# Two hybrid blocks on one core: neighbourhood attention by heads instead of by column tiles, and two projections interleaved

## The chip, the cores and the metric

One core of a Trainium2 chip runs the whole program. The metric is the device time of one execution in microseconds. Of the kernel before there are three timed executions and one profiled one.

## The reference

A sequence of 512 rows of 1024 goes through two blocks. The first block is a gated linear recurrence and a sliding-window attention with 16 heads. The second block runs two attentions side by side, mixes them with gates, and ends in an MLP. In float32, shortened:

```python
z = rms_norm(x, norm_mix) @ w_in          # q_a k_a v_a q_b k_b v_b g_a g_b
y_a = windowed_gqa(q_a, k_a, v_a, sink)   # 8 heads of 64, 2 kv heads, |distance| <= 128, blocks of 128
y_b = neighborhood_attn(q_b, k_b, v_b, rpb)  # 8 heads of 64 over a grid of 8 x 64; 8 x 16 neighbours
gates = sigmoid(concat([g_a, g_b]) + b_gate)
merged = gates[:, :1024] * (y_a @ w_proj_a) + gates[:, 1024:] * (y_b @ w_proj_b)
x = x + merged @ w_out
x = x + square(relu(rms_norm(x, norm_mlp) @ w_up)) @ w_down
```

The grid of the neighbourhood attention has 8 rows, so every row sees all 8 rows, and only the 16 columns around its own.

## The kernel before

**Number form.** Each float32 operand of a product is split into a high part (`rb`, float32r) and the rest, a low part. A product is three matmuls (`mm3`: high x high, high x low, low x high) into one PSUM bank. `split` makes the two parts: the high one mostly on ACT, the low one on DVE.

**Order of the work.** The program is written as many small generators that yield operations. `Sched.run` (a list scheduler) picks among them by its own costs and priorities while the program is built and fixes the order of each engine. One generator, `main`, goes through the list of matrix products (`jobs`) strictly in order, for example `block2` for the second block. Attention units, evacuations and weight loads are generators of their own, whose operations fall between. `Slots` hands out the buffers: 62 slots of 128 x 512 in `rb`, 38 in `fb`, 8 PSUM banks. A generator that finds no free slots waits. Weights come by DMA into `fb`, become high (`hi_task`, POOL or ACT) and low (`lo_task`, DVE) in `rb`, in the order of the products.

**Attention.** `attn_unit` handles four score tiles of 128 queries at a time: Q·K on PE, mask and maximum on DVE, exp on ACT, 1/sum on POOL, transposes of the probabilities on PE, their split (ACT, DVE), then the products P·V (`pv`) and `evac`. At most `MAXU = 4` units are under way. For the sliding-window heads (`swa_unit`) and the windowed heads (`a_unit`) a unit is a group of four heads and one block of 128 queries. V lies there in two arrangements (`v_heads`, `dup`) so that heads of either half of the partitions come out in place, and P·V is done in two column halves of 256 (`pv_groups`).

The neighbourhood heads come in four pairs (`pr`). The 512 positions are sorted into four column tiles (`ct`) of 16 grid columns. The outer tiles 0 and 3 see two key tiles, the inner ones 1 and 2 see three. A unit (`b_unit`) is a pair of heads with either the two outer or the two inner tiles; each P·V there is three matmuls of 256 columns (high and low part of V by high and low part of P, without low x low).

**End of block 2.** `block2` runs the projections `w_pa` (of the windowed heads) and `w_pb` (of the neighbourhood heads), eight outputs of 128 rows each with four k-steps. `pa_evac` multiplies with the gate, `pb_evac` multiplies, adds both, and splits the merged row (STT line L360, TT line L346) for `w_out_2`. `gemm_open` opens several outputs with the first k-steps and finishes them later, so that the last pair of heads may come late.

Lines that the text speaks of: L396 matmuls, L420 transposes, L322 ACT, L331 POOL copy of weights, L346 DVE tensor_tensor, L360 DVE scalar_tensor_tensor, L374 POOL multiplication, L389 reciprocal, L980 mask and maximum, L426 DMA.

Of the kernel before, what the change touches and what calls it, by code (L numbers as in the profile page):

```python
# [247 lines left out]
def kernel(ctx: ExitStack, tc: tile.TileContext, io: dict, out: bass.AP):  # L248
# [704 lines left out]
    def attn_unit(cfg):  # L953

        inflight[0] += 1
        nk = cfg["nk"]
        nkb = nk // P
        np_ = 2 if nk <= 256 else 3
        pair = nk <= 256
# [51 lines left out]
        for h in range(4):  # L1011
            yield A(pt[:, h, 0:nk], pt[:, h, 0:nk], AF.Exp, bias=nm[:, h:h + 1], accum=dn[:, h:h + 1])
# [4 lines left out]
        for h in range(4):  # L1017
            yield PMUL(pt[:, h, 0:nk], pt[:, h, 0:nk], rc[:, h:h + 1])
# [847 lines left out]
```

## Time and profile before

| | us |
|---|---|
| timed executions | 1155.03, 1154.68, 1152.27 |
| median | 1154.68 |
| profiled execution, its own time | 1149.55 |
| span of the profiled execution | 1147.7 |
| PE busy | 1126.9 (98%) |
| PE weight loads busy | 942.2 (82%) |
| DVE busy | 758.6 (66%) |
| ACT busy | 385.9 (34%) |
| POOL busy | 296.1 (26%) |
| mean granted clock of TensorE | 0.995 |

How to read it: the engines work at the same time and each in its own fixed order. An engine that isn't the bound may wait at no cost. Matmuls are pipelined, so the busy time of a single one is longer than the distance between two. Rough places in the span: the recurrence to about 240, the sliding-window attention to about 405, its output projection and the start of block 2 to about 460, the attentions of block 2 to about 720, the end of block 2 to about 790, then the MLP.

### The profile page before, as it was taken

The numbers are of one execution on the slowest core, as the hardware profiler recorded it, in microseconds if no ns is written. First come the engines' busy times: TensorE is split into PE (matmuls) and PEld (weight loads), VectorE is DVE, ScalarE is ACT, GpSimd is POOL, SyncE is SP. The second block draws the span as 40 slices with busy tenths as digits, with TensorE's granted clock in tenths as the row PEclk, the third lists the DMA queues.
The fourth block names the chain that finished last, engine by engine and source line by source line (L and its number), as shares of the span: only waits on it lengthen the run. The fifth ranks groups of instructions, "written<-read, shape, count | busy, mean of one in ns | idle before, by whom it ended". The sixth has DMA issues, their size and how long they took to land.

```text
span 1147.7 us, 14995 instructions
## 1 busy us (share of the span) xinstructions
PE 1126.9 (98%) x5468; PEld 942.2 (82%) x5468; DVE 758.6 (66%) x1335; ACT 385.9 (34%) x782; POOL 296.1 (26%) x392
## 2 busy tenths in 40 slices
PE   9999999999999999999999999899999999999997
PEld 6788888888888778888888788688888888888887
DVE  7999999675787896657765554876654324555332
ACT  5456761234665621166352233211111111111101
POOL 1222332125577422034132222312110002112110
PEclk9999999999999999999999999999999999999999
DMA  7243445208222512811553452622333222233001
GB/s 287 87 127 107 130 137 193 74 1 239 53 91 88 167 63 56 239 56 56 170 162 86 147 150 88 198 82 94 92 110 128 93 76 91 85 97 110 1 1 74
DMA packets 46794, 125.86 MB, mean 110 GB/s; under 512 B 6272, under 2 KB 7936, under 8 KB 46720
## 3 DMA queue, kind: packets, MB, share of 16 engines
q1 hardware_dynamic: 46720, 124.90, 34.7%
q8 instruction: 43, 0.70, 0.3%
q14 instruction: 31, 0.25, 0.1%
HBM read 104.95 MB, written 2.10 MB: 93 GB/s over the span
## 4 chain that ended last, share of the span: by engine, by line
PE 87%; DVE 5%; DMA 2%; issue 2%; POOL 1%; ACT 1%; SPq 0%; POOLq 0%; DVEq 0%; ACTq 0%
PE ps L396 85%; PE ps L420 3%; DVE fb L360 2%; DVE rb L346 2%; DVE fb L346 1%; POOL fb L374 1%; DMA fb<-in_mk 1%; DMA rb<-rb 1%; DVE fb L980 0%; DMA fb<-in_w_out 0%; DVE rb L360 0%; ACT rb L322 0%; DMA fb<-in_x 0%; ACT fb L322 0%; SPq L426 0%
## 5 line engine op out<-in xcount | busy, mean ns | idle before, releaser
L396 PE MATMUL ps<-rb 128*128 128x512 f32 (+1 forms) x5008 | 1093.1, 377 | 11.8 <-DVE rb L360 3.7
L396 PEld LDWEIGHTS ps<-rb 128*128 128x128 f32 x5008 | 890.5, 189 | 186.0 <-DVE rb L360 5.8
L331 POOL TENSOR_SCALAR rb<-fb 128x1024 fp32r<-128x1024 f32 (+4 forms) x159 | 169.3, 1076 | 605.7 <-PE ps L396 465.5
L346 DVE TENSOR_TENSOR rb<-fb,rb 128x512 fp32r<-128x512 f32 (+5 forms) x301 | 285.9, 974 | 47.7 <-ACT rb L322 39.7
L322 ACT ACTIVATE rb<-fb 128x512 fp32r<-128x512 f32 (+4 forms) x134 | 99.0, 747 | 305.0 <-DVE fb L360 155.6
L346 DVE TENSOR_TENSOR fb<-ps,fb 128x512 f32<-128x512 f32 (+2 forms) x134 | 78.1, 584 | 155.4 <-PE ps L396 143.7
L346 DVE TENSOR_TENSOR fb<-fb 128x512 f32<-128x512 f32 (+1 forms) x120 | 89.7, 754 | 22.9 <-ACT rb L322 20.8
L374 POOL TENSOR_SCALAR fb<-fb,sm 128x256 f32<-128x256 f32 (+2 forms) x128 | 69.1, 561 | 116.3 <-DVE sm L389 97.1
L346 DVE TENSOR_TENSOR rb<-ps,rb 128x512 fp32r<-128x512 f32 (+1 forms) x92 | 58.6, 641 | 44.0 <-ACT rb L322 39.6
L322 ACT ACTIVATE rb<-ps 128x512 fp32r<-128x512 f32 (+1 forms) x92 | 50.9, 558 | 81.1 <-PE ps L420 63.3
L360 DVE SCALAR_TENSOR_TENSOR fb<-ps,fb 128x512 f32<-128x512 f32 x56 | 38.5, 687 | 59.2 <-PE ps L396 59.1
L322 ACT ACTIVATE fb<-fb,sm 128x256 f32<-128x256 f32 (+2 forms) x128 | 65.3, 512 | 28.0 <-DVE sm L368 23.5
L322 ACT ACTIVATE fb<-fb 128x512 f32<-128x512 f32 (+1 forms) x66 | 39.5, 612 | 92.4 <-DVE fb L346 73.2
L322 ACT ACTIVATE rb<-fb,vec 128x512 fp32r<-128x512 f32 x41 | 28.4, 719 | 103.1 <-DVE fb L346 101.1
L322 ACT ACTIVATE fb<-ps 64x256 f32<-64x256 f32 (+1 forms) x60 | 25.2, 423 | 79.7 <-PE ps L396 67.8
L420 PE MATMUL ps<-ident,fb 128*128 128x128 f32 x328 | 48.4, 272 | 1.3 <-DVE fb L1582 0.9
L420 PEld LDWEIGHTS ps<-ident,fb 128*128 128x128 f32 x328 | 39.4, 140 | 8.4 <-DVE fb L1582 1.1
L980 DVE CUSTOM_DVE_ANT_0 fb<-ps,fb 128x256 f32<-128x256 f32 (+1 forms) x64 | 28.6, 486 | 14.2 <-DMA fb<-in_mbe 7.3
L374 POOL TENSOR_SCALAR fb<-fb,sm_qt 128x256 f32<-128x256 f32 (+1 forms) x64 | 33.3, 546 | 2.2 <-DMA fb<-in_mk 2.1
L360 DVE SCALAR_TENSOR_TENSOR rb<-fb,vec,rb 128x512 fp32r<-128x512 f32 x41 | 30.5, 761 | 0.6 <-ACT rb L322 0.3
L360 DVE SCALAR_TENSOR_TENSOR fb<-fb,vec 128x512 f32<-128x512 f32 x36 | 30.8, 872 | 0.0
L980 DVE CUSTOM_DVE_ANT_0 fb<-ps,fb,sm_qs 128x256 f32<-128x256 f32 (+1 forms) x64 | 26.7, 444 | 5.7 <-PE ps L396 3.3
(83 smaller groups left out, 323.3 us busy)
## 6 DMA issues: line engine op xcount, KB each, us to landing
rb<-rb SPq DMA_DIRECT2D x128, 128.0 KB, 2.3
fb<-in_w_down SPq DMA_DIRECT2D x32, 512.0 KB, 3.7
fb<-in_w_in SPq DMA_DIRECT2D x31, 512.0 KB, 3.7
fb<-in_w_up SPq DMA_DIRECT2D x29, 512.0 KB, 3.5
fb<-in_a_w_in SPq DMA_DIRECT2D x22, 512.0 KB, 3.9
fb<-in_b_w_in SPq DMA_DIRECT2D x16, 512.0 KB, 4.6
fb<-in_a_w_out SPq DMA_DIRECT2D x8, 512.0 KB, 3.5
fb<-in_wg SPq DMA_DIRECT2D x8, 384.0 KB, 3.8
```

The costliest lines, as they stand in the source:

```text
L322: opts = [("ACT", dur, lambda: nc.scalar.activation(out=o, in_=i, func=fn, **kw), TABLES.get(fn))]
L331: lambda: nc.gpsimd.tensor_scalar(out=o, in0=i, scalar1=1.0, scalar2=1.0, op0=ALU.mult, op1=ALU.mult), None,
L346: lambda: nc.vector.tensor_tensor(out=o, in0=a, in1=b, op=op), None,
L360: lambda: nc.vector.scalar_tensor_tensor(out=o, in0=a, scalar=s, in1=b, op0=op0, op1=op1), None,
L374: lambda: nc.gpsimd.tensor_scalar(out=o, in0=a, scalar1=s, scalar2=1.0, op0=ALU.mult, op1=ALU.mult), None,
L396: nc.tensor.matmul(out=o, lhsT=l, rhs=r, start=st, stop=sp)
L420: nc.tensor.transpose(o, i, ident)
L980: nc.vector.tensor_tensor_reduce(out=pt[:, h, 0:nk], in0=PS[:, b, o0:o0 + nk], in1=m, scale=sc, scalar=-3.0e38, op0=ALU.add, op1=ALU.max, ...
```

## The change

1. **V in one arrangement.** `v_heads` makes the high parts of V and the low parts side by side (64 columns high, 64 low) and no second arrangement. So one P·V matmul yields high x P in one half of the partitions and low x P in the other, and `evac` adds the halves. `pv_all` does all 512 columns at once; `pv_groups` goes.
2. **Neighbourhood units by head.** `b_unit(pr, e)` is one head and all four column tiles. Its scores have 256, 384, 384 and 256 columns. Its transposes go by key tile (2, 3, 3 and 2 blocks). P·V takes V in the same one arrangement, key tile by key tile over the column tiles that see it; the first is widened to 512 columns, over zeros that POOL writes (`pad`). The two heads of a pair are added into one `fb` slot and split once. The mask of a head is one DMA of 128 x 1280; it needs 3 slots (2 before), and each unit's probabilities need 3 (2 or 3 before).
3. **Order at the end of block 2.** `w_pa` outputs 4 to 7 stood before the last pair of heads. Now output 4 stands behind the gates, and 5 to 7 alternate with `w_pb` outputs 4 to 7. The slots of `yas` are held to the end of `w_pb`.

The core of the diff:

```diff
-    def split(src, scale=None, s=None):
-        if s is None:
...
+    def split(src, scale=None, n=T):
+        s = yield from ra.get(2)
+        h, l = RB[:, s, 0:n], RB[:, s + 1, 0:n]
+        yield A(h, src, AF.Copy, scale=scale, also="copy" if scale is None and not in_psum(src) else None)
...
     def v_heads(src, dst):
         b = yield from transposed(src)
-        s = yield from ra.get(4)
+        s = yield from ra.get(2)
         i = p_(b).rearrange("p (n e) -> p n e", e=64)
-
-        def dup(d):
-            return RB[:, s + 2 * d:s + 2 * d + 2, :].rearrange("p a (b v e) -> p (a b) v e", v=2, e=64)
-
-        h = dup(0)[:, :, 0, :]
-        yield A(h, i, AF.Copy)
-        yield TT(dup(0)[:, :, 1, :], i, asf(h), ALU.subtract)
-        yield A(dup(1)[:, :, 1, :], i, AF.Copy)
-        yield TT(dup(1)[:, :, 0, :], i, asf(h), ALU.subtract)
+        o = RB[:, s:s + 2, :].rearrange("p a (b v e) -> p (a b) v e", v=2, e=64)
+        yield A(o[:, :, 0, :], i, AF.Copy)
+        yield TT(o[:, :, 1, :], i, asf(o[:, :, 0, :]), ALU.subtract)
         pa.free(b)
         dst["v"] = s
 
-    def v_lhs(s, d, blk, kv):
+    def v_lhs(s, blk, kv):
         c = (blk * 2 + kv) * P
-        return RB[:, s + 2 * d + c // T, c % T:c % T + P]
+        return RB[:, s + c // T, c % T:c % T + P]
...
-        for hh in groups:
+        for hh in cfg["groups"]:
             b = yield from pa.get()
             lst = []
-            for h in hh:
+            for x, h in enumerate(hh):
                 l, kh, kl, k0, kn = cfg["item"](h)
-                o0 = (h % 2) * 256 if pair else 0
-                o = PS[:, b, o0:o0 + kn]
+                o = PS[:, b, x * 256:x * 256 + kn]
...
         ptr = []
-        for kb in range(nkb):
+        for x, lst in enumerate(cfg["trs"]):
             b = yield from pa.get()
-            yield TRS([(PS[:, b, i * P:(i + 1) * P], pt[:, h, kb * P:(kb + 1) * P]) for i, h in enumerate(cfg["order"])])
-            if kb == nkb - 1:
+            yield TRS([(PS[:, b, i * P:(i + 1) * P], pt[h][:, kb * P:(kb + 1) * P]) for i, (h, kb) in enumerate(lst)])
+            if x == len(cfg["trs"]) - 1:
                 fa.free(psl, np_)
-            s = yield from split(p_(b))
+            s = yield from split(PS[:, b, 0:len(lst) * P], n=len(lst) * P)
             pa.free(b)
             ptr.append(s)
+            if x == cfg.get("pad"):
+                z = RB[:, s, len(lst) * P:T]
+                yield Op([("POOL", 210.0, lambda: nc.gpsimd.memset(asf(z), 0.0), None)], [], [z])
         ob = yield from pa.get()
-        for c0, c1, vs in cfg["pv"]():
-            o = PS[:, ob, c0:c1]
-            for kb in range(nkb):
-                ph, pl = r_(ptr[kb])[:, c0:c1], r_(ptr[kb] + 1)[:, c0:c1]
-                if len(vs[kb]) == 2:
-                    yield MMS(mm3(o, *vs[kb], ph, pl, kb == 0, kb == nkb - 1))
-                else:
-                    c = cost(c1 - c0)
-                    yield MMS([
-                        (o, vs[kb][0], ph, kb == 0, False, c), (o, vs[kb][0], pl, False, kb == nkb - 1, c)
-                    ])
+        for kb, c0, c1, v, st, sp in cfg["pv"]():
+            w = T if st else c1 - c0
+            yield MMS([
+                (PS[:, ob, c0:c0 + w], v, RB[:, ptr[kb], 0:w], st, False, cost(w)),
+                (PS[:, ob, c0:c1], v, RB[:, ptr[kb] + 1, 0:c1 - c0], False, sp, cost(c1 - c0)),
+            ])
         for s in ptr:
             ra.free(s, 2)
         yield from cfg["evac"](ob)
         inflight[0] -= 1
...
+    def pv_all(s, kbs, kv):
+        n = len(kbs)
+        return [(x, 0, T, v_lhs(s, b, kv), x == 0, x == n - 1) for x, b in enumerate(kbs)]
...
-        r = yield from split(p_(b))
+        r = yield from ra.get(2)
+        i = p_(b).rearrange("p (n e) -> p n e", e=64)
+        o = RB[:, r:r + 2, :].rearrange("p a (b v e) -> p (a b) v e", v=2, e=64)
+        yield A(o[:, :, 0, :], i, AF.Copy)
+        yield TT(o[:, :, 1, :], i, asf(o[:, :, 0, :]), ALU.subtract)
...
-    def b_unit(pr, inner):
-        cts = (1, 2) if inner else (0, 3)
...
+    def b_unit(pr, e):
+
+        kt0 = (0, 0, 1, 2)
+        nkt = (2, 3, 3, 2)
+        cols = [(0, 256), (256, 384), (640, 384), (1024, 256)]
+
+        def item(ct):
             ks = kb_[pr] + 2 * e
-            return r_(qb[pr] + e)[:, ct * P:(ct + 1) * P], r_(ks), r_(ks + 1), kt0[ct] * P, nk
+            return r_(qb[pr] + e)[:, ct * P:(ct + 1) * P], r_(ks), r_(ks + 1), kt0[ct] * P, nkt[ct] * P
...
+            m = FB[:, mk2[pr, e]:mk2[pr, e] + 3, :].rearrange("p a t -> p (a t)")
+            return lambda ct: m[:, cols[ct][0]:cols[ct][0] + cols[ct][1]]
...
+            lst = []
+            for kt in (1, 0, 2, 3):
+                cts = [ct for ct in range(4) if kt0[ct] <= kt < kt0[ct] + nkt[ct]]
+                c = (kt * 2 + e) * P
+                v = RB[:, vb[pr] + c // T, c % T:c % T + P]
+                lst.append((kt, cts[0] * P, (cts[-1] + 1) * P, v, kt == 1, kt == 3))
+            return lst
...
+            if pr not in ybt:
+                ybt[pr] = None
+                ybt[pr] = yield from fa.get()
+            yield lambda: ybt[pr] is not None
+            f = ybt[pr]
+            o = FB[e * 64:e * 64 + 64, f, :].rearrange("p (r c i) -> p c r i", r=8, c=4, i=16)
+            v = [PS[h * 64:h * 64 + 64, ob, :].rearrange("p (c r i) -> p c r i", c=4, r=8) for h in range(2)]
+            yield A(o, v[1 - e], AF.Copy)
+            yield TT(o, v[e], o, ALU.add)
             pa.free(ob)
-            fa.free(mk2[pr, inner], 2)
+            fa.free(mk2[pr, e], 3)
             cntb[pr] = cntb.get(pr, 0) + 1
...
+                s = yield from split(f_(f))
+                fa.free(f)
+                ybs[pr] = s
+                yb[pr] = hilo(s)
...
+            "np": 3, "pad": 1, "cols": cols, "groups": ((0, 3), (1,), (2,)),
+            "trs": [[(ct, kt - kt0[ct]) for ct in range(4) if kt0[ct] <= kt < kt0[ct] + nkt[ct]] for kt in range(4)],
+            "sink": None, "item": item, "mask": mask, "scale": None, "pv": pv, "evac": evac,
...
-            for inner in (False, True):
+            for e in range(2):
                 yield from unit_slot()
-                mk2[pr, inner] = s = yield from fa.get(2)
...
+                mk2[pr, e] = s = yield from fa.get(3)
+                yield DMA(FB[:, s:s + 3, :].rearrange("p a t -> p (a t)")[:, 0:1280], io["mb"][2 * pr + e])
+                S.spawn(attn_unit(b_unit(pr, e)), 2)
...
         grid_heads(2)
-        proj_a(4, 8)
         grid_heads(3)
...
         for j in range(10, 16):
             z(18 + j, g2_evac, 3)
         then(lambda: free_acts(act_m))
+        proj_a(4, 5)
         gemm_open("w_pb", [0, 1, 2, 3], 3, 4, yb, pb_evac)
         for j in range(4, KD):
             gemm("w_pb", j, 4, yb, pb_evac, prio=1)
+            if j < KD - 1:
+                proj_a(j + 1, j + 2)
 
         def done_b():
+            for hg in range(2):
+                ra.free(yas[hg], 4)
             fa.free(n_m.bc)
             for pr in range(4):
                 ra.free(ybs[pr], 2)
```

What this makes of PE's order, at three places. In these rows `L396` are matmuls (`ps<-rb`, columns behind it), `L420` transposes.

End of the first block's attention, PE, before: the last P·V products of the sliding window (256 columns), the output projection, and the sums of the next norm (`ones,fb`).

```order
L420 MATMUL ps<-ident,fb 128x128 x4
L396 MATMUL ps<-rb 128x256 x4
L396 MATMUL ps<-rb 128x512 x3
L396 MATMUL ps<-rb 128x256 x8
L396 MATMUL ps<-rb 128x512 x6
L396 MATMUL ps<-rb 128x256 x6
L396 MATMUL ps<-rb 128x512 x147
L396 MATMUL ps<-ones,fb 128x1 x4
```

The same place of the change. P·V has 512 columns here and can't be told from the projection by its width; counted by PSUM bank in the built program, the last one is the 15th of the 183.

```order
L420 MATMUL ps<-ident,fb 128x128 x4
L396 MATMUL ps<-rb 128x512 x5
L420 MATMUL ps<-ident,fb 128x128 x8
L396 MATMUL ps<-rb 128x512 x8
L420 MATMUL ps<-ident,fb 128x128 x4
L396 MATMUL ps<-rb 128x512 x183
L396 MATMUL ps<-ones,fb 128x1 x4
```

Between the last P·V and the norm's sums stood 147 matmuls, and now stand 168.

End of the attentions of block 2, PE, before: the last unit (transposes of its three key tiles, 18 products of 256 columns), then what is left of `w_pb`, `w_out_2`, and the first of `w_up` up to the sums of the norm.

```order
L420 MATMUL ps<-ident,fb 128x128 x4
L396 MATMUL ps<-rb 128x512 x9
L420 MATMUL ps<-ident,fb 128x128 x4
L396 MATMUL ps<-rb 128x512 x9
L420 MATMUL ps<-ident,fb 128x128 x4
L396 MATMUL ps<-rb 128x512 x9
L396 MATMUL ps<-rb 128x256 x18
L396 MATMUL ps<-rb 128x512 x282
L396 MATMUL ps<-ones,fb 128x1 x4
```

The same place of the change; the last unit is now one head.

```order
L420 MATMUL ps<-ident,fb 128x128 x3
L396 MATMUL ps<-rb 128x512 x6
L420 MATMUL ps<-ident,fb 128x128 x2
L396 MATMUL ps<-rb 128x512 x7
L396 MATMUL ps<-rb 128x384
L396 MATMUL ps<-rb 128x256 x2
L396 MATMUL ps<-rb 128x384 x2
L396 MATMUL ps<-rb 128x256 x2
L396 MATMUL ps<-rb 128x512 x381
L396 MATMUL ps<-ones,fb 128x1 x4
```

The unit's P·V is one matmul of 512 columns (the last of the 7), three of 384 and four of 256, where a unit had 18 (or 12) of 256. Behind it stand 381 matmuls, 99 more: what is left of a gate and all of `w_pa` 4 to 7 and `w_pb`.

## Rows read from the trace of the kernel before

**Rows 1.** The page, busy time: us, share of the span, instructions.

```profile
PE 1126.9 (98%) x5468; PEld 942.2 (82%) x5468; DVE 758.6 (66%) x1335; ACT 385.9 (34%) x782; POOL 296.1 (26%) x392
```

**Rows 2.** Windows of five stretches, all engines; columns in the first line, clock as share.

```profile
core 0: us, PE busy (x) PEld busy (x) DVE busy (x) ACT busy (x) POOL busy (x), PEclk, DMA share, GB/s
240.00:405.00 165.00, 163.05 (x913) 139.97 (x913) 122.81 (x331) 91.24 (x250) 95.08 (x165) 1.00 0.38 115
404.00:413.00 9.00, 6.94 (x22) 4.74 (x21) 7.66 (x10) 1.59 (x3) 4.12 (x5) 0.81 0.19 64
500.00:720.00 220.00, 219.00 (x1176) 187.82 (x1175) 133.78 (x301) 86.05 (x210) 65.59 (x99) 1.00 0.38 115
735.00:745.00 10.00, 6.54 (x21) 4.18 (x20) 8.47 (x12) 1.89 (x3) 3.27 (x3) 0.83 0.72 247
408.60:412.10 3.50, 3.50 (x10) 2.42 (x9) 3.15 (x4) 0.72 (x1) 0.71 (x2) 0.52 0.42 142
```

**Rows 3.** Timeline of PE, end of the first block's attention: start, us, work [idle before].

```profile
406.20 0.50 PE L396 MATMUL ps<-rb 128*128 128x512 f32 x1 [0.49 <-ACT rb L322]
408.27 3.94 PE L396 MATMUL ps<-rb 128*128 128x512 f32 x9 [1.57 <-DVE rb L346]
```

**Rows 4.** Timeline of PE, end of block 2.

```profile
737.65 0.98 PE L396 MATMUL ps<-rb 128*128 128x512 f32 x3 [2.16 <-DVE rb L360]
...
741.26 3.93 PE L396 MATMUL ps<-rb 128*128 128x512 f32 x12 [0.47 <-DVE rb L360]
```

**Rows 5.** Groups of PE by form: busy us, mean ns | idle before.

```profile
L396 PE MATMUL ps<-rb 128*128 128x512 f32 x4248 | 999.8, 393 | 10.0 <-DVE rb L360 3.7 <-DVE rb L346 3.0 <-DMA rb<-rb 1.6
L396 PE MATMUL ps<-rb 128*128 128x256 f32 x696 | 101.4, 287 | 0.0
...
L396 PE MATMUL ps<-rb 128*128 128x384 f32 x64 | 15.7, 341 | 1.8 <-DMA rb<-rb 1.0 <-DVE sm L980 0.8
```

**Rows 6.** Chain that ended last, two pieces of the MLP: start, us, what.

```profile
741.26 370.72 PE ps L396 x1632
...
1114.36 6.47 PE ps L396 x54
```

**Rows 7.** Timeline of DVE, end of block 2.

```profile
718.40 0.86 DVE L346 TENSOR_TENSOR rb<-ps,rb 64x256 fp32r<-64x256 f32 x2 [3.11 <-ACT rb L322]
...
728.60 0.68 DVE L346 TENSOR_TENSOR rb<-fb,rb 128x512 fp32r<-128x512 f32 x1
729.21 0.68 DVE L346 TENSOR_TENSOR fb<-fb 128x512 f32<-128x512 f32 x1
729.81 0.68 DVE L360 SCALAR_TENSOR_TENSOR rb<-fb,rb 128x512 fp32r<-128x512 f32 x1
730.41 0.67 DVE L360 SCALAR_TENSOR_TENSOR fb<-fb,ps 128x512 f32<-128x512 f32 x1
```

**Rows 8.** Groups by form, 460 to 745 us: count, busy us, mean ns.

```profile
L346 DVE TENSOR_TENSOR rb<-fb,rb 128x1024 fp32r<-128x1024 f32 x29 | 35.5, 1231 | 0.5 <-ACT rb L322 0.4
L346 DVE TENSOR_TENSOR rb<-ps,rb 128x512 fp32r<-128x512 f32 x44 | 30.1, 689 | 28.1 <-ACT rb L322 24.5 <-DMA rb<-rb 3.5
...
L331 POOL TENSOR_SCALAR rb<-fb 128x1024 fp32r<-128x1024 f32 x22 | 23.9, 1094 | 95.6 <-PE ps L396 64.7 <-DVE sm L980 11.8 <-DMA fb<-in_w_out 8.6
```

**Rows 9.** DMA issues: KB each, median us from issue to landing.

```profile
fb<-in_w_in SPq DMA_DIRECT2D x31, 512.0 KB, 3.7
...
fb<-in_mbe SPq DMA_DIRECT2D x4, 512.0 KB, 3.9
...
fb<-in_mk SPq DMA_DIRECT2D x2, 768.0 KB, 6.9
```

**Rows 10.** Waits of DVE, 460 to 745 us: us in total, times, longest.

```profile
DVE fb L980 <- DMA fb<-in_mbe: 7.3, 4, 3.7
```

**Rows 11.** Timeline of PE at 385 us.

```profile
384.99 0.50 PE L396 MATMUL ps<-rb 128*128 128x512 f32 x1 [0.72 <-DVE rb L326]
385.92 1.42 PE L396 MATMUL ps<-rb 128*128 128x512 f32 x5 [0.43 <-DVE rb L346]
```

More of the change, by code (lines that the diff above doesn't have):

```diff
@@ L615, in wait_norm @@
         yield lambda: nrm.bc is not None
-    def split(src, scale=None, s=None):
-        if s is None:
-            s = yield from ra.get(2)
-        yield A(r_(s), src, AF.Copy, scale=scale, also="copy" if scale is None and not in_psum(src) else None)
+    def split(src, scale=None, n=T):
+        s = yield from ra.get(2)
+        h, l = RB[:, s, 0:n], RB[:, s + 1, 0:n]
+        yield A(h, src, AF.Copy, scale=scale, also="copy" if scale is None and not in_psum(src) else None)
         if scale is None:
-            yield TT(r_(s + 1), src, asf(r_(s)), ALU.subtract)
+            yield TT(l, src, asf(h), ALU.subtract)
         else:
-            yield STT(r_(s + 1), src, scale, asf(r_(s)), ALU.mult, ALU.subtract)
+            yield STT(l, src, scale, asf(h), ALU.mult, ALU.subtract)
         return s
@@ L955, in attn_unit @@
         inflight[0] += 1
[L956 to L959, printed above, removed]
+        np_ = cfg["np"]
         yield cfg["ready"]
         psl = yield from fa.get(np_)
-        pt = FB[:, psl:psl + np_, :].rearrange("p a t -> p (a t)").rearrange("p (h c) -> p h c", h=4)
+        flat = FB[:, psl:psl + np_, :].rearrange("p a t -> p (a t)")
+        pt = [flat[:, c:c + n] for c, n in cfg["cols"]]
         mx, nm, es, dn, rc = (small(4) for _ in range(5))
@@ L1043, in attn_unit, with even @@
         inflight[0] -= 1
-    def pv_groups(s, kbs, kv):
-        return [(e * 256, e * 256 + 256, [(v_lhs(s, e, b, kv),) for b in kbs]) for e in range(2)]
+    def even(nk, order):
+        w = 256 if nk <= 256 else 384
+        return {
+            "np": w * 4 // T, "cols": [(h * w, nk) for h in range(4)],
+            "groups": ((0, 1), (2, 3)) if nk <= 256 else ((0,), (1,), (2,), (3,)),
+            "trs": [[(h, kb) for h in order] for kb in range(nk // P)],
+        }
+    def pv_all(s, kbs, kv):
+        n = len(kbs)
+        return [(x, 0, T, v_lhs(s, b, kv), x == 0, x == n - 1) for x, b in enumerate(kbs)]
     def halves(ob, e):
@@ L1187, in swa_unit @@
         return {
-            "nk": nk, "sink": hg * 4, "order": (0, 2, 1, 3), "item": item, "mask": mask, "scale": stat(0), "std": stat(1), "pv": pv,
+            **even(nk, (0, 2, 1, 3)), "sink": hg * 4, "item": item, "mask": mask, "scale": stat(0), "std": stat(1), "pv": pv,
             "evac": evac,
@@ L1242, in done @@
             ra.free(kvb.pop("k"), 4)
-            ra.free(kvb.pop("v"), 4)
+            ra.free(kvb.pop("v"), 2)
         then(done)
@@ L1372, in evac @@
                     ra.free(kva.pop("k"), 4)
-                    ra.free(kva.pop("v"), 4)
+                    ra.free(kva.pop("v"), 2)
         return {
-            "nk": nk, "sink": 16 + hg * 4, "order": (0, 2, 1, 3), "item": item, "mask": mask, "scale": None, "pv": pv, "evac": evac,
+            **even(nk, (0, 2, 1, 3)), "sink": 16 + hg * 4, "item": item, "mask": mask, "scale": None, "pv": pv, "evac": evac,
             "ready": lambda: "k" in kva and "v" in kva and all(i in qa for i in q),
@@ L1406, in evac @@
-        def evac(ob):
-            if pr not in ybs:
-                ybs[pr] = None
-                ybs[pr] = yield from ra.get(2)
-            yield lambda: ybs[pr] is not None
-            s = ybs[pr]
-            def dst(x, e):
-                v = RB[e * 64:e * 64 + 64, x, :].rearrange("p (r c i) -> p c r i", r=8, c=4, i=16)
-                return v[:, 1:3] if inner else v[:, 0:4:3]
-            def src(e):
-                return half_view(ob, e).rearrange("p c (r i) -> p c r i", r=8)
-            for e in range(2):
-                yield A(dst(s, e), src(e), AF.Copy)
-            for e in range(2):
-                yield TT(dst(s + 1, e), src(e), asf(dst(s, e)), ALU.subtract)
+            lst = []
@@ L1513, in block2 @@
         grid_heads(2)
-        proj_a(4, 8)
         grid_heads(3)
-        def done_a():
-            for hg in range(2):
-                ra.free(yas[hg], 4)
-        then(done_a)
         for j in range(10, 16):
```

62 lines of the change are left out of this document (16 added, 46 removed).

## The prediction

> **What bounds it now.** I read the totals first: PE is busy for 98% of the span, DVE for 66%, ACT for 34% [rows 1]. The lesson to take from this is that only two kinds of change can move the end: less PE time, or fewer stretches in which PE stands still. So next I looked at the stages by themselves. In the attention of block 2 (500 to 720 us) PE is busy for 219.00 of 220.00 us while DVE has 133.78 and ACT 86.05; in that of the first block (240 to 405) PE has 163.05 of 165.00 [rows 2]. Both are matmul-bound, and what DVE and ACT do there is covered. Then I looked for the places where PE stands still, and two stand out, each at the end of an attention stage. From 404 to 413 PE is busy for 6.94 of 9.00 us and from 735 to 745 for 6.54 of 10.00, in both with a mean granted clock below 1 [rows 2]. The timeline of PE names who is waited for: DVE nearly each time, ACT once [rows 3, 4].
>
> **The price of a matmul.** The mean durations of the rows (393, 341 and 287 ns for 512, 384 and 256 columns) overlap, so they are no price [rows 5]. Long unbroken stretches of one width are: 370.72 us for 1632, nearly all 512 wide, is 0.2272 each, and 6.47 us for 54 of 256 columns is 0.1198 [rows 6]. For 384 I take the middle, 0.1735 (an estimate: the three means are 54 and 52 apart). Two halves cost 0.2396, one whole 0.2272: joining saves little, dropping products saves much.
>
> **Term 1, the products P·V.** The three-product form and the two column halves go.
> - First block: 4 groups x 7 key blocks x 4 = 112 matmuls of 256 become 56 of 512: 12.72 - 13.42 = -0.69 us.
> - Windowed heads of block 2: 2 x 10 x 4 = 80 become 40: -0.50.
> - Neighbourhood heads: a pair of heads had 12 + 18 = 30 of 256, so 120 in all. Now each of 8 units has one of 512, three of 384, four of 256: 8 x 0.2272 + 24 x 0.1735 + 32 x 0.1198 = 9.81 against 14.38: -4.56.
>
> Together 280 fewer of 256, 24 more of 384, 104 more of 512: **-5.75 us**. Q·K stays (32 of 256 and 32 of 384 on either side), and so do the transposes (80 for these units). PE is the engine of these stages, so I count the term in full. The Trainium skill (TensorE: Matmul & The Clock Gate, Back-to-back issue gap) gives a spacing of N/2.4 + 2.5 ns for an isolated matmul on the fast clock; by it, 109, 162 and 216 ns, the term would be about -4.2. The stretches measure some 11 ns more at each width, so the rows decide.
>
> **Term 2, the end of the first block's attention.** The output projection opens with six of eight k-steps for four outputs and then needs the last two heads' rows. Before, 12 matmuls stand between the last P·V and that need (2.7 us). PE waits 0.49 and 1.57 us [rows 3], and then runs 3.5 us at a clock of 0.52 [rows 2], which is nearly all at the lower of its two levels (1.2 against 2.4 GHz). In 9.00 us it did 22 matmuls, worth 22 x 0.2272 = 5.0: 4.0 us lost. In the new order the last P·V is the 15th of a run of 183, so 168 matmuls are left up to the sums of the norm, where there were 147. That is 21 more, and 4.8 us of cover against 2.1 of waiting. With the wait the slow stretch should go too: **-4.0 us**. If the chain through ACT and DVE comes later than I think, it is 0.
>
> **Term 3, the end of block 2.** DVE has a row of work without a pause from 718.40 on [rows 7], and PE waits for its merged rows (`rb L360`), first at 737.65 and last at 741.26 [rows 4]. Ten microseconds held 21 matmuls, 4.8 us of work: 5.2 lost. Why is DVE late? Each w_pb output asks of it three operations of 0.68 (gate product, sum, low half) and a low half of a weight, also 0.68 [rows 7]: 2.7 us for an output whose 12 matmuls take 2.7 us. So DVE only keeps pace, and the 8.2 us that the first four outputs left behind them is never worked off. In the change a w_pa output stands between each two: 24 matmuls (5.45 us) for 2.04 + 0.68 + 2 x 0.68 = 4.1 of DVE. From the k-step of the last pair to the first need of the last merged row there are 12 + 84 + 36 + 9 = 141 matmuls, 32 us; DVE owes 8 x 2.04 + 3 x 0.68 + 13 low halves x 0.68 = 27 in it. That fits, though not by much, so I count **-4.5** of the 5.2. The four w_pa outputs cost PE the same 10.9 us wherever they stand.
>
> **What is added and costs nothing, with its cover.**
> - Splits: 32 narrower ones where there were 20 wide ones, and per pair one more of the sum. At 0.69 each on DVE as an upper bound [rows 8], 16 x 0.69 = 11 us; the four evacuations of a unit become two. DVE has 86 us free in that stage [rows 2]. Below nothing: the two v-halves per layer that fall away.
> - Eight fills of zeros on POOL: no row has one. Between nothing and 1.09 us, POOL's longest step there [rows 8]. I take nothing: two more groups of transposes and their splits stand between a fill and its reader.
> - Masks: eight DMAs of 640 KB for four of 512 and four of 384. Those of 512 land in 3.9 us, those of 768 in 6.9 [rows 9]; between them I estimate 5.4, 1.5 later. DVE stood 7.3 us in all before such masks [rows 10], and PE was still busy for 219.00 of 220.00. So nothing; were all eight to reach PE, 12 us. That is an end of the range only for the case with late weights below.
> - SP issues as many DMAs as before; the w_pa weights are only later in its queue.
>
> **Sum.** -5.75 - 4.0 - 4.5 = -14.3 us. The profiled execution took 1149.55 us (span 1147.7), so this makes 1135.3 there; the median of the runs lies 5.1 higher, at 1154.68. The difference carries over: **1140.4**.
>
> **Rivals.**
> 1. *One stall moves instead of going.* For: both end in a DVE chain, and term 3 leaves DVE 5 us of slack in 32. Against: the covers above. Then -5.75 - 4.0 or -5.75 - 4.5: 1144.4 to 1144.9.
> 2. *Only the products count.* PE reaches both ends sooner and waits the longer, since DVE's work is as long as it was. Then -5.75: 1148.9. Against: at both places the order itself is longer, by 21 and by 99 matmuls.
> 3. *The weights starve, and it is slower.* Place: the third and fourth pair. Of 38 slots for fp32 data, 8 hold x, 1 the norm and 10 gates, so 19 are left. A unit now takes 6 (mask 3, probabilities 3), where it took 4 or 5; three units leave 1, and a weight needs 2 side by side. A weight that is issued only when needed costs its landing, 3.7 us [rows 9], a POOL step of 1.09 and a DVE step of 1.23 [rows 8]: 6.0. From three such waits on (18 against 14.3) the kernel is slower: 1158.4. Against: in the new order the tightest weight of that stretch is still issued 109 matmuls ahead of its use (an output of the gates; counted in the built program). The Trainium skill (Trainium Kernel Development and Optimization, Best Practices) warns that consistent bubbles can mean that SBUF or PSUM ran out; the 219.00 of 220.00 say that it hasn't so far.
> 4. *More than the sum*: PE also waits 0.72 and 0.43 us at 385 for the two parts of a weight that DVE makes [rows 11]; if that goes too, and all of term 3, 1140.4 - 1.15 - 0.7 = 1138.5.
>
> That the change doesn't do what it says is no rival here: the counts of each width and the 99 matmuls more behind the last P·V stand in the built order.
>
> **How the numbers follow.** The forecast and its near neighbourhood (rival 4 included) get 0.62, rival 1 0.18, rival 2 0.11, rival 3 0.05, and 0.04 is left for gains that meet a smaller new wait and end within 0.3%, which is about what a measurement of this kernel can tell from no change (3.5 us). Rivals 1 and 2 are still faster, so faster is 0.91, same 0.04, slower 0.05. The range takes in rivals 1 and 2 above and, below, rival 4 with some 4 us more, the width of the three runs shown (1152.27 to 1155.03) and a few small gaps: 1134 to 1150.
>
> **What would show it.** Term 1: 416 matmuls of 256 columns, 88 of 384, 4352 of 512, and PE busy less by about 6 us beside the two ends. Term 2: no wait of PE for DVE between the last P·V of the first block and its norm, and a clock of 1.00 there. Term 3: no wait for `rb L360` where w_out_2 begins, and DVE with pauses in the stretch of w_pb. I am wrong if PE shows a new wait of over 2 us, above all one for a weight's low half in the last two pairs, or if the clock falls at another place.

## The result and the profile after

| | before | after |
|---|---|---|
| median, timed side by side, 4 executions each (us) | 1153.47 (1150.38 to 1155.03) | 1137.34 (1136.91 to 1139.50) |
| ratio of the times | | 0.9876, 95% interval 0.985 to 0.9903 |
| profiled execution, own time / span | 1149.55 / 1147.7 | 1139.5 / 1137.7 |

The changed kernel is faster by 1.24% by this ratio, which is an estimate of its own with its interval; the two medians divided make 0.986, inside the interval. The forecast was 1140.4 against 1154.68, a ratio of 0.9876 as well, and 1137.34 lies in its range. That the sum was right does not yet mean that each of its terms was; the traces show two of the three otherwise than foretold.

The page of the changed kernel, busy times (us, share of the span, instructions), against [rows 1], and its masks against [rows 9]:

```profile
PE 1119.6 (98%) x5316; PEld 931.7 (82%) x5316; DVE 758.7 (67%) x1344; ACT 384.1 (34%) x781; POOL 306.6 (27%) x404
...
fb<-in_mb SPq DMA_DIRECT2D x8, 640.0 KB, 5.9
```

PE is busy for 7.3 us less, and still for 98% of a shorter span. The windows of [rows 2], with one more at 386:

```profile
core 0: us, PE busy (x) PEld busy (x) DVE busy (x) ACT busy (x) POOL busy (x), PEclk, DMA share, GB/s
240.00:405.00 165.00, 160.47 (x835) 134.51 (x836) 121.77 (x328) 90.35 (x248) 99.44 (x167) 0.98 0.36 112
404.00:413.00 9.00, 9.00 (x42) 7.44 (x41) 6.57 (x10) 1.02 (x3) 2.89 (x4) 1.00 0.51 175
500.00:720.00 220.00, 220.00 (x1106) 185.34 (x1105) 145.29 (x325) 93.06 (x227) 67.11 (x107) 1.00 0.43 131
735.00:745.00 10.00, 10.00 (x46) 8.28 (x45) 4.16 (x6) 0.72 (x1) 2.60 (x3) 1.00 0.26 91
386.00:393.00 7.00, 5.25 (x16) 3.79 (x17) 6.47 (x15) 5.00 (x16) 6.21 (x11) 0.62 0.71 252
```

Both holes of [rows 2] are closed: PE works through 404 to 413 and 735 to 745 at a clock of 1.00. But in the first block, from 240 to 405, it is now busy for 160.47 us where it was 163.05, at 0.98 where it was 1.00. The last line says why: between 386 and 393 it did 16 matmuls at a clock of 0.62. That hole is new.

When the sums of the two norms stand in the timeline of PE tells which stage gained. First before, then after:

```profile
440.44 0.95 PE L396 MATMUL ps<-ones,fb 128*128 128x1 f32 x8
...
786.96 0.94 PE L396 MATMUL ps<-ones,fb 128*128 128x1 f32 x8
```

```profile
441.51 0.95 PE L396 MATMUL ps<-ones,fb 128*128 128x1 f32 x8
...
776.93 0.95 PE L396 MATMUL ps<-ones,fb 128*128 128x1 f32 x8
```

The end of the first block did not come earlier (441.51 for 440.44). Between the two norms lie 335.42 us where there were 346.52, and behind the second 1137.7 - 776.93 = 360.8 where there were 360.7. So all of the gain between these two traces is in block 2.

### The profile page after: what moved, and what is told of

Its sections match the earlier page's. It is cut to its first block, busy times and chain, and to the rows that moved or that the text cites. A ratio compares the mean times of both kernels' runs of the same rounds, so it can differ in the third digit from the quotient of the medians.

```text
span 1137.7 us, 14747 instructions
## 1 busy us (share of the span) xinstructions
PE 1119.6 (98%) x5316; PEld 931.7 (82%) x5316; DVE 758.7 (67%) x1344; ACT 384.1 (34%) x781; POOL 306.6 (27%) x404
## 4 chain that ended last, share of the span: by engine, by line
PE 93%; DVE 2%; issue 2%; DMA 1%; ACT 1%; POOL 1%; SPq 0%; POOLq 0%; DVEq 0%
PE ps L396 90%; PE ps L420 3%; DVE fb L360 1%; DMA fb<-in_mk 1%; POOL fb L374 0%; DMA fb<-in_x 0%; DVE rb L346 0%; SPq L426 0%; ACT rb L322 0%; DVE fb L346 0%; ACT fb L322 0%; DMA rb<-rb 0%; DVE fb L972 0%; DVE fb L1632 0%; POOLq L1846 0%
## 5 line engine op out<-in xcount | busy, mean ns | idle before, releaser
L396 PE MATMUL ps<-rb 128*128 128x512 f32 (+2 forms) x4856 | 1087.1, 383 | 5.1 <-DMA rb<-rb 1.6
L396 PEld LDWEIGHTS ps<-rb 128*128 128x128 f32 x4856 | 878.0, 188 | 177.6 <-issue 3.0
L331 POOL TENSOR_SCALAR rb<-fb 128x1024 fp32r<-128x1024 f32 (+5 forms) x163 | 175.5, 1087 | 564.2 <-PE ps L396 407.4
L346 DVE TENSOR_TENSOR rb<-fb,rb 128x1024 fp32r<-128x1024 f32 (+5 forms) x305 | 289.0, 972 | 40.9 <-ACT rb L322 37.1
L346 DVE TENSOR_TENSOR fb<-ps,fb 128x512 f32<-128x512 f32 (+3 forms) x142 | 83.6, 590 | 156.7 <-PE ps L396 141.0
L374 POOL TENSOR_SCALAR fb<-fb,sm 128x256 f32<-128x256 f32 (+2 forms) x128 | 74.9, 603 | 125.3 <-DVE sm L389 97.1
L360 DVE SCALAR_TENSOR_TENSOR fb<-ps,fb 128x512 f32<-128x512 f32 x56 | 38.5, 688 | 58.4 <-PE ps L396 58.3
L346 DVE TENSOR_TENSOR rb<-ps,rb 128x512 fp32r<-128x512 f32 (+2 forms) x86 | 52.3, 612 | 37.5 <-ACT rb L322 35.5
L322 ACT ACTIVATE rb<-ps 128x512 fp32r<-128x512 f32 (+2 forms) x86 | 46.0, 538 | 82.1 <-PE ps L420 73.8
L322 ACT ACTIVATE fb<-ps 64x256 f32<-64x256 f32 (+2 forms) x68 | 30.1, 442 | 82.5 <-PE ps L396 72.4
L420 PE MATMUL ps<-ident,fb 128*128 128x128 f32 x328 | 52.3, 276 | 5.4 <-POOL fb L374 4.5
L420 PEld LDWEIGHTS ps<-ident,fb 128*128 128x128 f32 x328 | 41.3, 142 | 17.2 <-POOL fb L374 6.2
L360 DVE SCALAR_TENSOR_TENSOR rb<-fb,vec,rb 128x512 fp32r<-128x512 f32 x41 | 30.5, 763 | 0.6 <-ACT rb L322 0.4
L360 DVE SCALAR_TENSOR_TENSOR fb<-fb,vec 128x512 f32<-128x512 f32 x36 | 30.2, 856 | 0.0
```

Source lines behind the costliest of these rows:

```text
L322: opts = [("ACT", dur, lambda: nc.scalar.activation(out=o, in_=i, func=fn, **kw), TABLES.get(fn))]
L331: lambda: nc.gpsimd.tensor_scalar(out=o, in0=i, scalar1=1.0, scalar2=1.0, op0=ALU.mult, op1=ALU.mult), None,
L346: lambda: nc.vector.tensor_tensor(out=o, in0=a, in1=b, op=op), None,
L360: lambda: nc.vector.scalar_tensor_tensor(out=o, in0=a, scalar=s, in1=b, op0=op0, op1=op1), None,
L374: lambda: nc.gpsimd.tensor_scalar(out=o, in0=a, scalar1=s, scalar2=1.0, op0=ALU.mult, op1=ALU.mult), None,
L396: nc.tensor.matmul(out=o, lhsT=l, rhs=r, start=st, stop=sp)
```

## The experiments

**Two further traces, of the kernel before and of the changed one**, no edit.

> The kernel before once more, unchanged, for a second trace. Open is which stretch makes the spread of its executions (1150.4 to 1155.0 us). If the wait at the end of the first block's attention varies, the sums of the norm behind it (440.44 us in the first trace) move by some 2 to 4 us while the stages before and behind keep their length; if it is spread over all stages, none moves by more than 1 us.

> The changed kernel once more, unchanged, for a second trace. My theory: the wait of TensorE for GpSimd's multiplications at 384 to 390 us belongs to the new order and comes again, 5 to 9 us lost there, and the span is 1135 to 1138. The rival: it was an accident of one execution; then under 3 us are lost there and the span is under 1134.

They took 1152.93 and 1137.93 us. The second trace of before, timeline of PE:

```profile
482.46 5.74 PE L396 MATMUL ps<-rb 128*128 128x384 f32 x27 [2.90 <-DVE sm L980]
```

The sums of the norms stood 349.5 us apart, three more than in the first trace, and the first block's end moved by 0.4 us only (440.88). Of these three, 2.1 are the wait for the first mask of block 2, 2.90 us where it was 0.81 there. So neither expectation came true for these two traces: what parts them is not the wait at 404, and it is not spread over all stages either. In the changed kernel the new hole was there again, in a span of 1136.1 us. Its waits of PE from 372 to 413 us (in total, times, longest), the only ones:

```profile
PE ps L420 <- POOL fb L374: 4.3, 4, 1.6
```

**E1, the order alone.** The kernel before, with the order at the end of block 2 of the change.

```diff
         grid_heads(2)
-        proj_a(4, 8)
         grid_heads(3)
...
+        proj_a(4, 5)
         gemm_open("w_pb", [0, 1, 2, 3], 3, 4, yb, pb_evac)
         for j in range(4, KD):
             gemm("w_pb", j, 4, yb, pb_evac, prio=1)
+            if j < KD - 1:
+                proj_a(j + 1, j + 2)
...
```

> The kernel before with only the new order of the w_pa outputs. My theory (the end of block 2 waited for VectorE, and spacing the w_pb outputs cures it): faster by 4.5 to 5.5 us, ratio 0.995 to 0.996, and no wait for rb L360 where w_out_2 begins. The rival (the units by head take the load off VectorE, the order alone moves the wait elsewhere): within 1.5 us of before, ratio 0.999 to 1.001.

Measured: 1143.13 us against 1149.97, ratio 0.9937 (0.9921 to 0.9954), by which it is some 7.2 us (6.8 by the medians), more than was expected. Its timeline of PE:

```profile
636.72 10.45 PE L396 MATMUL ps<-rb 128*128 128x512 f32 x50
...
699.82 50.48 PE L396 MATMUL ps<-rb 128*128 128x512 f32 x222
```

222 matmuls in a row, from 700 to 750: no wait for `rb L360` is left, so term 3 is a thing of the order and needs nothing of the new units. Its size was set too low. The wait went whole, which is 5.2 us and not 4.5. Further, at 636.72 PE runs on where the kernel before waited for a DMA from `rb` to `rb`, here in that kernel's timeline:

```profile
641.94 5.37 PE L396 MATMUL ps<-rb 128*128 128x384 f32 x26 [0.98 <-DMA rb<-rb]
```

5.2 and 0.98 make 6.2, inside the interval (5.3 to 9.1 us); the last microsecond has no row of its own.

**E2, the new attention with the old order.** The changed kernel, with the lines of E1 turned back.

```diff
         grid_heads(2)
+        proj_a(4, 8)
         grid_heads(3)
...
-        proj_a(4, 5)
         gemm_open("w_pb", [0, 1, 2, 3], 3, 4, yb, pb_evac)
         for j in range(4, KD):
             gemm("w_pb", j, 4, yb, pb_evac, prio=1)
-            if j < KD - 1:
-                proj_a(j + 1, j + 2)
...
```

> The changed kernel with the old place of w_pa outputs 4 to 7, in front of the last pair of heads. My theory: the wait at the end of block 2 is back (5 us, with a stretch at half clock), so this run is 4.5 to 5.5 us slower than the changed kernel and some 9 to 11 faster than before, ratio 0.990 to 0.992. The rival (units by head alone cure the end): no such wait, as fast as the changed kernel, ratio 0.987 to 0.988.

Measured: 1145.0 us, ratio 0.9953 (0.9936 to 0.997), some 5.4 us. That is term 1 (5.75) without the 4.0 of term 2, and so less than was expected. The wait at the end of block 2 is back, in its timeline of PE (the first row is the sums of the first norm):

```profile
439.94 0.95 PE L396 MATMUL ps<-ones,fb 128*128 128x1 f32 x8
...
730.92 0.96 PE L396 MATMUL ps<-rb 128*128 128x512 f32 x3 [3.15 <-DVE rb L360]
732.73 1.61 PE L396 MATMUL ps<-rb 128*128 128x512 f32 x3 [0.85 <-DVE rb L360]
```

PE goes on from it 6.7 us earlier than in [rows 4], since PE got there sooner, and 3.15 us are waited where it was 2.16. This is the prediction's second rival on a small scale: a part of what the products save is waited away again here.

What the products save can be read up to this wait, since the jobs of block 2 come in the order of before there. From the sums of the first norm to where the wait begins PE takes 730.92 - 3.15 - 439.94 = 287.83 us in E2, with no wait in between. Before, it took 737.65 - 2.16 - 440.44 = 295.05 us, of which 1.79 were waits (0.81 for the mask, 0.98 for the DMA; [rows 5] has them in one), so 293.26 without them. That is 5.4 us less, where the sum had 4.56 + 0.50 = 5.06 for block 2.

E1 and E2 together save 0.63% + 0.47% = 1.10%, against 1.24% (0.97 to 1.5) of the whole change: within the intervals the two halves add up, and no third part is needed. (The wait of 0.98 is gone in both runs, so their sum counts it twice.)

**The changed kernel again, and E3, V in one arrangement alone.** E3 is the kernel before with `v_heads`, `v_lhs` and P·V of 512 columns as in the change, with neither the units by head nor the new order.

> The changed kernel itself, timed again beside the next three on one chip, with a third trace. The first two traces lost 8.9 and 7.7 us of TensorE's time between 380 and 400 us. If that belongs to the order it comes a third time; the ratio to before should lie between 0.985 and 0.990 again.

```diff
-        s = yield from ra.get(4)
+        s = yield from ra.get(2)
...
+        o = RB[:, s:s + 2, :].rearrange("p a (b v e) -> p (a b) v e", v=2, e=64)
+        yield A(o[:, :, 0, :], i, AF.Copy)
+        yield TT(o[:, :, 1, :], i, asf(o[:, :, 0, :]), ALU.subtract)
...
-        return [(e * 256, e * 256 + 256, [(v_lhs(s, e, b, kv),) for b in kbs]) for e in range(2)]
+        return [(0, T, [(v_lhs(s, b, kv),) for b in kbs])]
```

> The kernel before with the one arrangement of V and the P.V products over 512 columns for the sliding-window and the windowed heads, but the old units of the neighbourhood heads and the old order of w_pa. TensorE's order in the first block is that of the changed kernel. My theory: the wait of TensorE for GpSimd at 384 to 390 is there, the wait of 4 us at 404 to 412 is gone, and the stage keeps its length; ratio 0.998 to 1.001, that is 0 to 2 us faster. The rival (the prediction's term 2: cover alone decides): 4 to 6 us faster, ratio 0.995 to 0.9965.

Measured: the changed kernel 1138.07 us, ratio 0.9893 (0.9865 to 0.992), with the hole a third time; E3 1150.33 against 1150.98, ratio 0.9999 (0.9985 to 1.0013). E3 gains nothing, and it shows where term 2 went. From its timeline of PE and a window:

```profile
385.05 0.33 PE L420 MATMUL ps<-ident,fb 128*128 128x128 f32 x1 [1.62 <-POOL fb L374]
386.46 1.28 PE L420 MATMUL ps<-ident,fb 128*128 128x128 f32 x4 [1.09 <-POOL fb L374]
388.91 0.69 PE L420 MATMUL ps<-ident,fb 128*128 128x128 f32 x2 [1.17 <-POOL fb L374]
...
399.83 12.45 PE L396 MATMUL ps<-rb 128*128 128x512 f32 x54
...
441.13 0.95 PE L396 MATMUL ps<-ones,fb 128*128 128x1 f32 x8
...
386.00:393.00 7.00, 4.96 (x17) 3.46 (x18) 6.33 (x15) 5.71 (x19) 6.21 (x11) 0.53 0.61 212
```

The wait at 404 to 409 is gone, as term 2 had it: 54 matmuls run through. But 20 us earlier PE now waits at the transposes of the last units for the probabilities that POOL still has to multiply with 1/sum, and the low clock (0.53) follows there. The sums of the first norm stand at 441.13, no earlier than before (440.44). The stall moved; it did not go.

**E4, POOL relieved.** If POOL's multiplications are what PE waits for, sharing them with ACT should close the hole. In the changed kernel, the sliding-window units may have either engine multiply:

```diff
+    def PAMUL(o, a, s):
+        op = PMUL(o, a, s)
+        op.opts.append((
+            "ACT", 286.0 + 0.833 * _free(o),
+            lambda: nc.scalar.activation(out=o, in_=a, func=AF.Copy, scale=s), None,
+        ))
+        return op
...
-                yield PMUL(pt[h], mask(h), cfg["std"](h))
+                yield PAMUL(pt[h], mask(h), cfg["std"](h))
...
-            yield PMUL(pt[h], pt[h], rc[:, h:h + 1])
+            yield (PMUL if scale is None else PAMUL)(pt[h], pt[h], rc[:, h:h + 1])
```

> The changed kernel, where the scheduler may give the two multiplications of a sliding-window score tile (mask by deviation, probabilities by 1/sum) to ScalarE as well as to GpSimd. My theory: GpSimd's backlog from 358 to 372 makes the last units late; with part of it on ScalarE less than 3 us are lost between 372 and 412 (8 to 9 now), and the run is 3 to 6 us faster than the changed kernel. The rival (VectorE, busy for 18.3 of 20 us from 372 to 392, is the bound there): the loss stays over 5 us and the time within 2 us of the changed kernel's.

Measured: 1133.51 us, ratio 0.9852 (0.9826 to 0.9878), 4.6 us less than the changed kernel beside it, and the fastest version of all. Its windows, and the waits of PE from 372 to 413:

```profile
372.00:413.00 41.00, 38.96 (x180) 30.94 (x181) 36.26 (x75) 22.64 (x63) 20.05 (x24) 1.00 0.44 151
386.00:393.00 7.00, 6.75 (x33) 5.41 (x34) 5.13 (x15) 4.42 (x11) 3.55 (x6) 1.00 0.88 314
...
PE ps L404 <- DVE rb L346: 1.3, 3, 0.5
PE ps L404 <- DVE rb L326: 1.0, 1, 1.0
```

(Its lines stand 8 further down: L404 is L396.) No wait for POOL is left and the clock stays at 1.00; from 386 to 393 PE does 33 matmuls where it did 16. The 4.6 us are about the 4.0 that term 2 had promised, and they lie where it put them: the sums of the first norm come at 436.12, in the three traces of the changed kernel at 440.32 to 442.84. The rival, that DVE is the bound there, does not fit: from 372 to 392 DVE is busy for 18.03 of 20.00 us here and for 18.34 in the changed kernel, and the loss went all the same. What this does not show is that POOL's number of multiplications alone was to blame, since the new choice also gave the scheduler another plan.

**E8, the same relief for the kernel before.** The edit of E4 in the old units. Had both stalls one origin, the wait at 404 should shrink.

> The kernel before with the two multiplications of a sliding-window score tile open to ScalarE as well as GpSimd. My theory: the wait of before at 404 to 412, which the prediction put down to too little cover, came from the same late units as the changed kernel's wait at 384; so before too loses less between 372 and 413 (some 6 us there now) and gets 2 to 5 us faster, ratio 0.9955 to 0.998. The rival: its wait at 404 is the evacuation's own chain on ScalarE and VectorE behind the last product, with only 12 matmuls to cover it; then it stays, and the ratio is 0.999 to 1.001.

Measured: 1161.44 us, ratio 1.0089 (1.0071 to 1.0107), slower, which neither the theory nor the rival had. Its waits of PE from 372 to 430:

```profile
PE ps L404 <- ACT rb L322: 6.8, 2, 4.5
PE ps L404 <- DVE rb L346: 1.7, 2, 0.9
```

Now PE waits for ACT, up to 4.5 us at once. So what was a relief in one plan was a load in the other, and whether both stalls have one origin stays open.

**E6, the four outputs in one block.** Is it the alternation, or only the work that stands behind the last pair of heads? In E6 as many matmuls stand there as in the change (381), but `w_pa` 4 to 7 in a block ahead of `w_pb`.

```diff
-        proj_a(4, 5)
+        proj_a(4, 8)
         gemm_open("w_pb", [0, 1, 2, 3], 3, 4, yb, pb_evac)
         for j in range(4, KD):
             gemm("w_pb", j, 4, yb, pb_evac, prio=1)
-            if j < KD - 1:
-                proj_a(j + 1, j + 2)
```

> The changed kernel with w_pa outputs 4 to 7 in one block behind the gates and in front of w_pb, not alternating with it; as many matmuls (381) stand behind the last unit as in the changed kernel. My theory (each w_pb output asks of VectorE as much time as TensorE takes for it, so they must be spaced): a wait for rb L360 where w_out_2 begins is back, 3 to 6 us lost, and the run is 3 to 7 us slower than the changed kernel, ratio to before 0.992 to 0.995. The rival (it is enough that the last unit ends earlier): no wait there, ratio as the changed kernel's, 0.987 to 0.990.

Measured: 1147.04 us against 1152.08, ratio 0.9961 (0.9942 to 0.998). Its timeline of PE, its window from 700, and the pauses of its DVE ahead of the stretch of `w_pb` and behind it:

```profile
732.91 1.65 PE L396 MATMUL ps<-rb 128*128 128x512 f32 x3 [3.88 <-DVE rb L360]
...
700.00:745.00 45.00, 40.81 (x166) 32.11 (x165) 29.31 (x42) 5.05 (x8) 10.82 (x11) 0.92 0.42 146
...
715.08 0.69 DVE L360 SCALAR_TENSOR_TENSOR fb<-fb,ps 128x512 f32<-128x512 f32 x1 [4.93 <-PE ps L396]
746.68 0.69 DVE L346 TENSOR_TENSOR fb<-ps,fb 128x512 f32<-128x512 f32 x1 [7.95 <-PE ps L396]
```

The wait is all there, 3.88 us, and DVE works through the whole stretch of `w_pb`, from 715.08 to 738.7, without a pause. E6 equals E2 within the intervals, so moving the block behind the attentions gains nothing; it is the spacing between two `w_pb` outputs that gains. That it would be this little was not expected (0.992 to 0.995 was).

**E5, the first mask sooner.** The wait at 482 (1.50 us in the profiled execution of the changed kernel) is for the first mask of the windowed heads. E5 is the changed kernel that fetches it at the start of block 2.

```diff
         for hg in range(2):
-            yield lambda: 2 * hg in qa and 2 * hg + 1 in qa and "k" in kva
+            if hg:
+                yield lambda: 2 * hg in qa and 2 * hg + 1 in qa and "k" in kva
             mk2[hg] = s = yield from fa.get(3)
             yield DMA(FB[:, s:s + 3, :], io["mk2"][hg])
+            yield lambda: 2 * hg in qa and 2 * hg + 1 in qa and "k" in kva
...
+        then(lambda: S.spawn(driver2(), 2))
         first = {4: k2_evac, 5: v2_evac, 0: qa_evac}
...
-        then(lambda: S.spawn(driver2(), 2))
```

> The changed kernel with the first mask of block 2's windowed heads fetched when block 2 begins, not when its queries are there. TensorE's wait before the first 384-column scores at 480 us was 0.2 to 3.2 us in six traces, once with a stretch at half clock. If it waits for that mask, the wait goes to under 0.3 us and the median falls by 1 to 2 us with a smaller spread; if it waits for something else (the stacked keys or queries), it stays at 1 us or more.

Measured: 1139.64 us, ratio 0.9906 (0.988 to 0.9931), not to be told from the changed kernel beside it (0.9893). The wait for the mask is gone, and another stands in its place, in the timeline of PE:

```profile
469.25 15.08 PE L396 MATMUL ps<-rb 128*128 128x384 f32 x71 [0.93 <-DMA rb<-rb]
```

## Why the prediction was right, and where not

**What bounds it: held.** PE from 500 to 720 is busy for 220.00 of 220.00 us, the gains came from less PE time and from stalls, and where the stall only moved (E3) the time stayed.

**Term 1 (-5.75): held.** The groups of PE by form, against [rows 5]:

```profile
L396 PE MATMUL ps<-rb 128*128 128x512 f32 x4352 | 1024.3, 393 | 3.6 <-DMA rb<-rb 1.6 <-ACT rb L322 1.1 <-DVE rb L346 0.6
L396 PE MATMUL ps<-rb 128*128 128x256 f32 x416 | 60.5, 286 | 0.0
...
L396 PE MATMUL ps<-rb 128*128 128x384 f32 x88 | 22.8, 341 | 1.5 <-DVE sm L972 1.5
```

The counts are as foretold. E2's time, 5.4 us less (3.5 to 7.4), is not this term by itself, since the end of block 2 waits longer there; its rows are better, 5.4 us of PE's own work in block 2 against 5.06 in the sum. The estimate by the Trainium skill (TensorE: Matmul & The Clock Gate, Back-to-back issue gap), about -4.2 in all, would be some 4.1 in block 2 by the same spacings, so the rows decide for the measured prices. The joined products of the first block and the windowed heads, -1.19 in the sum, were too small to be measured in E3 (-0.1, between -1.7 and +1.5, which holds both nothing and -1.19).

**Term 2 (-4.0): failed; it is 0.** The step that failed is "21 more, and 4.8 us of cover against 2.1 of waiting". It counted what PE has to do behind the last P·V, and took for granted that PE gets to that P·V as before. The prediction's caveat, "if the chain through ACT and DVE comes later than I think, it is 0", named the case but the wrong engine and place: ahead of the last P·V stand transposes, and ahead of these POOL. The prediction's own sign of being wrong, "if the clock falls at another place", came true here. The changed kernel, timeline of POOL:

```profile
359.16 5.38 POOL L374 TENSOR_SCALAR fb<-fb,sm_qt 128x256 f32<-128x256 f32 x8
364.51 1.39 POOL L374 TENSOR_SCALAR fb<-fb,sm 128x256 f32<-128x256 f32 x3
365.87 4.11 POOL L374 TENSOR_SCALAR fb<-fb,sm_qt 128x256 f32<-128x256 f32 x8
369.96 2.55 POOL L374 TENSOR_SCALAR fb<-fb,sm 128x256 f32<-128x256 f32 x4
...
382.96 6.04 POOL L374 TENSOR_SCALAR fb<-fb,sm 128x256 f32<-128x256 f32 x8 [6.73 <-DVE sm L389]
```

and its timeline of PE:

```profile
379.85 2.57 PE L396 MATMUL ps<-rb 128*128 128x512 f32 x10
384.04 0.33 PE L420 MATMUL ps<-ident,fb 128*128 128x128 f32 x1 [1.62 <-POOL fb L374]
385.51 1.13 PE L420 MATMUL ps<-ident,fb 128*128 128x128 f32 x4 [1.15 <-POOL fb L374]
387.95 0.69 PE L420 MATMUL ps<-ident,fb 128*128 128x128 f32 x2 [1.32 <-POOL fb L374]
389.05 0.47 PE L420 MATMUL ps<-ident,fb 128*128 128x128 f32 x1 [0.41 <-POOL fb L374]
```

Read from the bottom up: the transposes wait, one by one, for eight multiplications that began at 382.96 and take 0.76 us each; these waited for DVE's reciprocals (`sm L389`), POOL standing idle for 6.73 us. Up to 372.5 POOL had 23 multiplications without a pause, of which the 16 with `sm_qt` prepare the masks of other units. The 4.5 us of waiting at 384 and the low clock to 393 took back what was won at 404. E3 shows that V's arrangement, with P·V in 512 columns, does this without the rest of the change; E4 shows that the term is there to be had. Which of the earlier steps made the reciprocals late, no run isolates.

**Term 3 (-4.5): the mechanism held, the size was too small.** E1 measured 7.2 us (5.3 to 9.1). No wait for `rb L360` is left, as foretold. DVE's pauses in the changed kernel, in its timeline:

```profile
709.13 0.69 DVE L360 SCALAR_TENSOR_TENSOR fb<-fb,ps 128x512 f32<-128x512 f32 x1 [4.52 <-PE ps L396]
...
730.21 0.69 DVE L360 SCALAR_TENSOR_TENSOR fb<-fb,ps 128x512 f32<-128x512 f32 x1 [0.79 <-PE ps L396]
...
741.09 0.69 DVE L346 TENSOR_TENSOR fb<-ps,fb 128x512 f32<-128x512 f32 x1 [5.70 <-PE ps L396]
```

Within the stretch of `w_pb`, from 709.13 to 735.4, DVE pauses for 0.21 and 0.79 us alone. The 4.52 us lie ahead of it and the 5.70 behind it, and E6 has two such pauses as well and yet waits. So "That fits, though not by much" is what the trace shows; the step that failed is "so I count -4.5 of the 5.2", since work that just fits leaves no wait, and all of the 5.2 came. And the wait of 0.98 for stacked keys, which went with it in E1, stood in no term. E6 confirms the argument behind the term (2.7 us of DVE for 2.7 us of matmuls per output, so no backlog is worked off) from the other side.

**What was to cost nothing: held.** The masks landed in 5.9 us (estimated 5.4), DVE waited for them 4.6 us in all where it was 7.3 [rows 10], and PE had none of it. POOL's eight fills took 0.206 us each, near the lower of the two ends.

```profile
DVE fb L972 <- DMA fb<-in_mb: 4.6, 5, 2.1
...
L1021 POOL MEMSET rb<- 128x128 f32 x8 | 1.6, 206 | 9.0 <-DVE rb L346 5.5 <-DMA rb<-rb 3.5
```

**The rivals.** Rival 1 (one stall moves) is what happened at the first place, rival 2 (PE comes sooner and waits the longer) what E2 shows at the second; for the whole kernel neither was right, because term 3 gave some 2.7 of the 4.0 that term 2 did not. Rival 3 (late weights) did not appear: in block 2 PE waited for no weight. So the forecast hit by two errors of opposite sign, +4.0 for term 2 and some -2.7 for term 3; of the rest, -5.75 is the part that the runs bear out as it was worked out.

There is a further piece of luck in the last step, "The difference carries over". The profiled execution went from 1149.55 to 1139.5, which is 10.05 us and not 14.3. Before, it lay 3.9 us below the median of the four timed executions; in the changed kernel it lies 2.2 above. The second pair of traces is 15.0 us apart. So one pair of traces is too few to test a sum of 14.3 us, and the agreement of the two ratios of 0.9876 to four digits is chance.

## What to carry to other kernels

Work that is put between a producer and its reader covers a wait only if the producer's own chain starts no later than before: follow it back through every engine (here transposes, POOL's multiplication, DVE's reciprocal) up to where the order changed, before the cover is counted. Where PE waits for an engine that just keeps pace, compare that engine's time per output with PE's, and spread other outputs between them; the same work in one block ahead gained nothing here. What joining two half-wide matmuls into one saves was too small to be measured here; what dropping products saves was not.

## What the runs showed of the hardware

Nearly the same wait may or may not be followed by the low clock. In the second trace of the kernel before PE waited 2.90 us at 482, in E1 3.07 at the same place, both after an unbroken run of matmuls of over 19 us. Windows of the one, and timeline of PE and windows of the other:

```profile
482.00:485.00 3.00, 2.54 (x14) 2.18 (x15) 3.00 (x15) 0.00 (x0) 0.00 (x0) 1.00 0.62 229
485.00:488.00 3.00, 3.00 (x15) 2.51 (x14) 3.00 (x11) 0.00 (x0) 0.00 (x0) 1.00 0.07 20
```

```profile
482.04 6.14 PE L396 MATMUL ps<-rb 128*128 128x384 f32 x22 [3.07 <-DVE sm L980]
...
482.00:485.00 3.00, 2.96 (x12) 2.44 (x13) 3.00 (x15) 0.00 (x0) 0.00 (x0) 0.75 0.61 229
485.00:488.00 3.00, 3.00 (x11) 2.57 (x11) 3.00 (x11) 0.00 (x0) 0.00 (x0) 0.68 0.17 27
```

In the first the clock stayed at 1.00; in the second it was 0.75 and then 0.68, that is, for a part of the time at 1.2 GHz, and 23 matmuls were done where the other did 29. The length of the wait alone does not decide: at 408 in the kernel before, waits of 0.49 and 1.57 us [rows 3], together shorter than the 2.90, were followed by 3.5 us at 0.52 [rows 2]. So a wait has a price in two parts, and of the second only a trace tells whether it is paid. The Trainium skill (TensorE: Matmul & The Clock Gate, What's actually happening) says that the activity is watched in a free-running way, not in step with the program. By that, the same wait can fall either way, and the rows above fit it; no run here shows the mechanism itself.
